# Low parts of weights by accumulating transfers onto ScalarE's negative, and a later place for a mean between two layers

## The chip, the cores and the metric

The kernel runs on one core of a Trainium2 chip. The metric is the device time of one execution in microseconds (us); the time of a kernel is the median of several executions.

## The reference

Two layers of an encoder, all in float32, with 512 tokens of width 1024 and 256 memory tokens:

```
for each layer:
  h   = rms_norm(x, g_pre)
  z   = h @ w_in                     # 1024 -> 5632: q, k, v of branches A and B, q of M, gates
  A   = neighborhood_attention(q, k, v, rpb)      # 6 heads, learned position bias rpb
  B   = dilated_attention(q, k, v)                # 3 groups of 2 heads, ALiBi distances
  M   = memory_attention(q, rms_norm(mem, mem_g), w_kv)
  y   = sigmoid-gated sum of A @ w_bra, B @ w_brb, M @ w_brm
  x   = x + rms_norm(y @ w_out, g_post)
  h   = rms_norm(x, g_pref)
  u   = gelu-gated MLP of h (w_up, a convolution of width 3 over positions, w_down)
  x   = x + rms_norm(u, g_postf)
```

rms_norm divides by the root of the mean of the squares over the 1024 channels.

## The kernel before

All activations are held transposed: channels on the 128 partitions, tokens along the free axis, in two halves of 256 tokens. A float32 product is made of three TensorE matmuls (`mm3`) in the type float32r: every operand is split into a high part (`hi`, the value rounded by ScalarE's copy) and a low part (`lo` = value - `hi`), and the product is hi x hi + hi x lo + lo x hi.

`weights` loads one block of a weight (1024 x 128, 512 KB) from DRAM on SyncE's queue into one of three buffers `wraw`. For blocks that are prepared ahead it then splits it in two chunks of 128 x 512 into tiles called `m`: ScalarE copies (`m<-wraw`, CAST) and an engine given by the argument `eng` subtracts (`m<-wraw,m`, L225 for GpSimd, L114 for VectorE: most of ScalarE's and VectorE's instructions have line 114, that of a wrapper that counts). In the names of the order lists below, m_71 and m_73 are the two high chunks of a block, m_72 and m_74 its low chunks.

GpSimd makes the low parts of three sets of blocks. In layer 0's first group, six blocks of w_in (`FIRST` = 0, 3, 4, 7, 6, 1), it makes the fourth and the sixth. Between the layers it makes those of the memory weights 2 and 3 (string `KVE`), and of the blocks 0, 1, 3 and 5 of layer 1's first group (string `GEN`; `G` is GpSimd, `V` VectorE); the first two of that group (`NG`) are prepared by the job `kv_ahead`, the others later.

TensorE's order is written out as the program is built: `Woven` keeps a clock that is an estimate in us, each matmul adds its cost, and jobs (generators) yield the time after which they want to go on; TensorE's instructions are chained in the order in which they are made. The other engines get their own instructions in an order that a scheduler chooses, each queue in order, with semaphores between them. GpSimd's queue holds its arithmetic and also the issue of its DMAs (a software queue): a DMA behind an instruction that waits is not issued before it.

The position bias of branch A is loaded by `a_bias` (L593 to L600), once for each head: a DMA of 128 KB on GpSimd's queue (`y<-in_rpb_dram`, L596), then three subtractions from a mask on GpSimd (`y<-mask,y`, L599). The load is held behind the last low part of a weight that GpSimd has made:

```
behind(nc.gpsimd.dma_start(out=raw, in_=rpb[l, h]).ins, last_lo.get(G))
```

`last_lo` is set in `split`, by the engine that subtracts. Its buffer is one of eight `y` tiles, which VectorE uses for the residual's product and for squares.

At the end of layer 0 (`end_job`, `raw_end_job`) the result of each half is normalised and added to the residual: transposes bring the statistics (`pt<-ident,st`), VectorE makes `y<-y,pt` and `x<-x,y` for eight channel blocks, ScalarE the squares of the new `x` (`sq<-x`), VectorE sums them (`acc<-acc,sq`), and TensorE takes their mean over channels by a matmul with a constant (`pt<-mean,acc`). For the second half, layer 1's first group of products goes on meanwhile with values that are not yet normalised (`ka`), and the mean's matmul stands among those products, where the job's `yield 3.5` puts it.

Of the kernel before, what the change touches and what calls it, by code (L numbers as in the profile page):

```python
# [9 lines left out]
AF = mybir.ActivationFunctionType  # L10
ALU = mybir.AluOpType
# [9 lines left out]
KD = D_MODEL // 128  # L21
# [6 lines left out]
FIRST = (0, 3, 4, 7, 6, 1)  # L28
# [6 lines left out]

LAT_QK, LAT_SM, LAT_T, LAT_V, LAT_T2 = 1.0, 4.5, 1.5, 2.0, 0.6
STEP_A, STEP_B, STEP_M = 9.0, 9.0, 5.5
SQG, LOG, GEN, KVE = {0: (), 1: ()}, {0: (), 1: ()}, 'GGVGVG', 'VVGG'
SD1 = 4.0
MARGIN = 0.3  # L40
SB = True
# [1 line left out]
KVD, GWD, NG, LAT1 = 7.3, 1.0, 2, 12.0  # L43
# [76 lines left out]
def tile_hybrid_encoder(ctx, tc, xT, memT, memg, vecs, rpb, w_in, w_kv, w_bra, w_brb, w_brm,  # L120
                        w_out, w_up, w_down, c_ident, c_mask, c_tab0, c_tab1, out):
    nc = tc.nc
# [13 lines left out]
    uid, last_copy, last_act, crit, last_lo = [0], [None], [None], [None], {}  # L136
    wv = Woven(tc)

    def nm(s):
        uid[0] += 1  # L140
        return f"{s}_{uid[0]}"


    def big(dt=F32R, shape=(128, 512)):
        return mp.tile(list(shape), dt, tag="m", name=nm("m"))
# [4 lines left out]
    def ktile(dt=F32R, shape=(128, 512)):  # L150
        return tp.tile(list(shape), dt, tag="ka", name=nm("ka"), bufs=12)
# [22 lines left out]
    def f32(ap):  # L174
        return ap.bitcast(F32)

    G = nc.gpsimd
    ACT, V = Counted(nc.scalar, wv, 0.1, 0.8e-3), Counted(nc.vector, wv, 0.065, 1.05e-3)

    DUP, MDUP = G, G  # L180
    MSQ = G

    def ready(least):
# [5 lines left out]
    def xh(k, half):  # L189
        return xs[:, half.start // 256, k, :]  # L190
# [27 lines left out]
    def behind(ins, other):  # L218

        if other is not None and ins is not other:  # L220
            tc.add_manual_dep(ins, other.name, ORDER, reason="issue order")

    def split(src, hi, lo, eng=None):
        last_copy[0] = ACT.copy(hi, src).ins
        last_lo[eng or V] = (eng or V).tensor_sub(lo, src, f32(hi)).ins  # L225

    def weights(src, K, C, slot=None, eng=None, after=None):

        raw = wp.tile([128, K, C], F32, tag="wraw", name=nm("wraw"))
        nc.sync.dma_start(out=raw, in_=src)  # L230
        if slot is None:
            hi = wp.tile([128, K, C], F32R, tag="whi", name=nm("whi"), bufs=2)
            lo = wp.tile([128, K, C], F32R, tag="wlo", name=nm("wlo"), bufs=2)
            split(raw, hi, lo, eng)
            behind(last_copy[0], after)
            return [(hi[:, k, :], lo[:, k, :]) for k in range(K)]
        n = 512 // C
        w = []
        for k in range(0, K, n):
            c = min(n, K - k)  # L240
            hi, lo = slot(F32R, (128, c, C)), slot(F32R, (128, c, C))
            split(raw[:, k:k + c, :], hi, lo, eng)
            w += [(hi[:, i, :], lo[:, i, :]) for i in range(c)]
        return w

# [68 lines left out]
    def sumsq_add(acc, src, first, slot=None, eng=None):  # L314
        if first:
            ACT.activation(acc, src, AF.Square)
        else:
            n = acc.shape[-1]
            sq = slot((128, 256)) if slot else small("sq2", 4) if n == 256 else small("sq", 1, (128, 512))
            ACT.activation(sq, src, AF.Square)  # L320
            (eng or V).tensor_add(acc, acc, sq)
# [4 lines left out]
    def rstd_job(accs, n, box):  # L326

        nb = n // 128
        bank = tbank((128, n + nb))
        pr, pt = bank[:, 0:n], bank[:, n:n + nb]  # L330
        for i, a in enumerate(accs):
            for b in range(nb):
                mm(pt[:, b:b + 1], a[:, 128 * b:128 * b + 128], mean, i == 0 and b == 0,
                   i == len(accs) - 1 and b == nb - 1, 0.11)
        rs = smalls(nb)
        crit[0] = ACT.activation(rs, pt, AF.Sqrt, bias=eps, scale=1.0).ins
        V.reciprocal(rs, rs)
        yield 0.8
        for b in range(nb):
            one = rs[:, b:b + 1]  # L340
            spread = bass.AP(one.tensor, one.offset, [list(one.ap[0]), [0, 128]])
            wv.pe(nc.tensor.transpose(pr[:, 128 * b:128 * b + 128], spread, ident), 0.11)
        box.append(pr)

    def normed(src, g, rs, hi, lo, eng=None):
        h32 = small("h32", 3)
        V.scalar_tensor_tensor(out=h32, in0=src, scalar=g, in1=rs, op0=ALU.mult, op1=ALU.mult)
        split(h32, hi, lo, eng)

    def raw_split(l, goff, k, src, hi, lo):  # L350

        g = vec[:, l, goff + k:goff + k + 1]
        ACT.activation(hi, src, AF.Copy, scale=g)
        V.scalar_tensor_tensor(out=lo, in0=src, scalar=g, in1=f32(hi), op0=ALU.mult, op1=ALU.subtract)

    def rtile():
        return tp.tile([128, 512], F32, tag="R", name=nm("R"), bufs=1)
# [60 lines left out]
    def raw_end_job(l, goff, og, acc, acc2, nxt, lat):  # L418


        half, box = HALVES[1], []
        hs, raw, R = nxt
        yield lat
        raw.extend((t[:, 0, :], t[:, 1, :]) for t in [ktile(F32R, (128, 2, 256)) for _ in range(KD)])
        yield from rstd_job([acc[:, half]], 256, box)
        for k in range(KD):
            V.tensor_mul(og[k][:, half], og[k][:, half], box[0])
            V.tensor_add(xh(k, half), xh(k, half), og[k][:, half])
            raw_split(l + 1, V_PRE, k, xh(k, half), *raw[k])
            if k == 0:  # L430
                yield 0.6
            wv.give(f"raw{k}")
            yield 1.05
        for k in range(KD):
            sumsq_add(acc2[:, half], xh(k, half), k == 0)
        yield 3.5
        box = []
        yield from rstd_job([acc2[:, half]], 256, box)
        ACT.copy(R[:, half], box[0])
        wv.give("R")  # L440
        for k in range(KD):
            normed(xh(k, half), vec[:, l + 1, V_PRE + k:V_PRE + k + 1], box[0], hs[k][0][:, half], hs[k][1][:, half])
        crit[0] = last_copy[0]
        yield 1.2
        wv.give(f"h{l + 1}.{V_PRE}.1")

    def h_tiles():
        return [(htile(), htile()) for _ in range(KD)]


    def mem_norm_job(l, hm, slot):
# [6 lines left out]
        for k in range(KD):  # L458
            sumsq_add(acc, raws[k], k == 0, None, MSQ if l else V)
        yield 14.0  # L460
# [34 lines left out]
    def group_weights(srcs, engs):  # L495
        return [weights(s, KD, 128, big, e) for s, e in zip(srcs, engs)]
# [19 lines left out]
    def proj(l, m, hs, after=None):  # L516
        w = weights(w_in[l, m], KD, 128, after=after)
        ps = mmbank()
        linear(ps, w, hs)
        return ps  # L520
# [366 lines left out]
    gw = group_weights([w_in[0, m] for m in FIRST[:2]], (V, V))  # L887
# [4 lines left out]
    with tc.issue_after(last_copy[0]):  # L892
        sqs = first_squares(HALVES[1])
    wv.spawn(pre_norm_job(0, V_PRE, sqs, hs, 1), SD1)
    gw += group_weights([w_in[0, m] for m in FIRST[2:]], (V, G, V, G))
    for t, c in ((mask, c_mask), (tab0, c_tab0), (tab1, c_tab1)):
        nc.sync.dma_start(out=t, in_=c)
    hm = []
# [3 lines left out]
    for l in range(depth):  # L902
# [41 lines left out]
        for m in range(KD):  # L944
# [3 lines left out]
            hi, lo = big(), big()  # L948
# [4 lines left out]
        hs, R, gw = h_tiles(), rtile(), []  # L953
# [44 lines left out]
        if l == depth - 1:  # L998
            sublayer_end(l, V_POSTF, w_of, fs, 2, None)
            while wv.jobs:  # L1000
                wv._step()
        else:
            hm, km, vm = [], [], []
            wv.spawn(mem_norm_job(l + 1, hm, htile), 20.0)
            pre, R, raw, box = [], rtile(), [], []

            def then(a, i, l=l, box=box):
                box.extend(h_tiles())
                return pre_norm_job(l + 1, V_PRE, a, box, i)

            gw = []

            def kv_ahead(l=l, pre=pre, gw=gw):
                pre.append(weights(w_kv[l + 1, 0], KD, 128, htile))
                yield KVD
                for i in (1, 2, 3):
                    yield 0.9
                    pre.append(weights(w_kv[l + 1, i], KD, 128, big, G if KVE[i] == 'G' else V))
                wv.give(f"kv{l + 1}")
                for m in range(NG):  # L1020
                    yield GWD
                    gw.extend(group_weights([w_in[l + 1, FIRST[m]]], [G if GEN[m] == 'G' else V]))
                wv.give(f"gw{l + 1}")

            sublayer_end(l, V_POSTF, w_of, fs, 1, [then, (box, raw, R)], (1.4, LAT1), lambda: wv.spawn(kv_ahead()))
            wv.need(f"kv{l + 1}")
            mem_kv(l + 1, hm, km, vm, pre)
            wv.need(f"gw{l + 1}")
            gw += group_weights([w_in[l + 1, m] for m in FIRST[NG:]], [G if e == 'G' else V for e in GEN[NG:]])
            wv.need(f"h{l + 1}.{V_PRE}.0")  # L1030
            hs = box

# [92 lines left out]
```

## Time and profile before

| what | value |
|---|---|
| median of 3 runs | 1551.14 us (1551.08 to 1551.52) |
| the profiled execution | 1551.73 us, its span 1550.0 us |
| mean granted TensorE clock in it | 0.995 |
| GpSimd's instructions and busy time | 217, 149.7 us |
| subtractions of weights on GpSimd near the start | 4, from 24.12 to 31.81 us |
| subtractions of weights on GpSimd between the layers | 8 from 768.30 to 780.85 us, 4 from 795.61 to 803.88 us |
| a bias load, from issue to landing | 2.3 least, 2.9 median, 7.0 most |

In the timeline rows of the profile the columns are the start in us, the length in us, the engine, the line, the operation with its tiles (written out<-in), the shape and how many instructions the row holds, and in brackets the idle time ahead of it with what ended it. PE is TensorE, DVE is VectorE, ACT is ScalarE, POOL is GpSimd and SP is SyncE. PEclk is the clock granted to TensorE, 1.00 being full speed.

### The profile page before, as it was taken

The page shows a single profiled execution, that of the slowest core. Times are in us where ns is not written, and L with a number is a line of the kernel's source. Part 1 is how long each engine was busy: PE and PEld are TensorE (multiplying, and loading weights), DVE is VectorE, ACT ScalarE, POOL GpSimd, SP SyncE. Part 2 cuts the span into 40 slices and gives each one's busy share as a digit, 9 for nine tenths or more (in the row PEclk, how much of TensorE's full clock was granted, in tenths as well). Part 3 has the DMA queues.
Part 4 walks back from the last instruction along what each step waited for, and adds up shares of the span by engine and source line. Part 5 has one row for each costly group of instructions (what it writes and reads, how often), then busy time and mean ns, then how long its engine had stood idle before and what let it go on. Part 6 is the DMA issues. An engine that isn't in the chain of part 4 may idle for free.

```text
span 1550.0 us, 20648 instructions
## 1 busy us (share of the span) xinstructions
PE 1522.5 (98%) x7970; PEld 1300.1 (84%) x7970; DVE 951.6 (61%) x1684; ACT 712.7 (46%) x1266; POOL 149.7 (10%) x217
## 2 busy tenths in 40 slices
PE   8999999999999999999989999999999999999997
PEld 7988888888988888888888888888889888888887
DVE  6685676335777777742497756753456977776233
ACT  5565554336544444532355555532354544444231
POOL 3340000110000000000154300002100000000000
PEclk9999999999999999999999999999999999999999
DMA  7221213235113322333431221132350233323331
GB/s 246 89 88 64 62 57 107 84 95 165 53 59 100 100 96 95 118 90 101 129 102 59 78 66 58 61 104 88 102 177 15 82 96 99 101 99 89 99 105 63
DMA packets 45810, 144.91 MB, mean 93 GB/s; under 512 B 5376, under 2 KB 9600, under 8 KB 45712
## 3 DMA queue, kind: packets, MB, share of 16 engines
q1 hardware_dynamic: 43776, 139.85, 28.5%
q10 hardware_dynamic: 1296, 2.10, 0.4%
q0 software_dynamic: 640, 1.64, 0.3%
q8 instruction: 62, 1.02, 0.3%
q14 instruction: 36, 0.29, 0.1%
HBM read 141.48 MB, written 2.10 MB: 93 GB/s over the span
## 4 chain that ended last, share of the span: by engine, by line
PE 91%; DVE 6%; ACT 2%; issue 1%; DMA 0%; SPq 0%; ACTq 0%; DVEq 0%
PE mm L247 80%; PE s L247 4%; PE o L247 3%; PE pt L258 2%; DVE m L114 1%; DVE y L114 1%; PE pt L247 1%; DVE ka L114 1%; DVE x L114 1%; ACT y L114 1%; DVE st L114 0%; DVE acc L114 0%; DMA x<-in_xT_dram 0%; DVE wlo L114 0%; ACT whi L114 0%
## 5 line engine op out<-in xcount | busy, mean ns | idle before, releaser
L247 PE MATMUL mm<-h,whi 128*128 128x512 f32 x2496 | 776.5, 392 | 0.0
L247 PEld LDWEIGHTS mm<-h,whi 128*128 128x128 f32 x2496 | 462.0, 188 | 91.3
L247 PE MATMUL mm<-h,wlo 128*128 128x512 f32 x1248 | 486.9, 390 | 0.0
L114 DVE TENSOR_TENSOR wlo<-wraw,whi 128x1024 fp32r<-128x1024 f32 (+1 forms) x213 | 259.2, 1217 | 284.7 <-ACT whi L114 282.3
L114 ACT CAST whi<-wraw 128x1024 fp32r<-128x1024 f32 (+1 forms) x213 | 221.4, 1040 | 307.8 <-PE mm L247 293.4
L247 PEld LDWEIGHTS mm<-h,wlo 128*128 128x128 f32 x1248 | 234.5, 188 | 49.6
L247 PE MATMUL mm<-m,whi 128*128 128x512 f32 (+1 forms) x800 | 215.1, 356 | 1.0 <-DVE m L114 0.8
L247 PEld LDWEIGHTS mm<-m,whi 128*128 128x128 f32 x800 | 141.8, 189 | 22.8 <-PE mm L247 1.3
L247 PE MATMUL mm<-m,wlo 128*128 128x512 f32 (+1 forms) x400 | 142.1, 355 | 0.0
L114 DVE SCALAR_TENSOR_TENSOR y<-y,vec,y 128x511 f32<-128x511 f32 x176 | 130.5, 748 | 3.5 <-ACT y L114 0.9
L114 DVE TENSOR_TENSOR y<-mm,R 128x512 f32<-128x512 f32 x82 | 56.4, 688 | 68.5 <-PE mm L247 68.5
L247 PEld LDWEIGHTS mm<-m,wlo 128*128 128x128 f32 x400 | 75.5, 189 | 10.9
L802 POOL TENSOR_TENSOR m<-m,y 128x512 f32<-128x512 f32 x28 | 36.1, 1289 | 399.4 <-DVE y L114 399.4
L114 ACT ACTIVATE y<-y,vec 128x512 f32<-128x512 f32 x88 | 71.1, 815 | 2.3 <-DVE y L114 1.9
L247 PE MATMUL mm<-m,m 128*128 128x512 f32 x240 | 63.5, 394 | 0.0
L114 ACT ACTIVATE y<-y 128x512 f32<-128x512 f32 x44 | 27.9, 633 | 71.7 <-DVE y L114 71.3
L114 ACT CAST m<-pt 128x512 fp32r<-128x512 f32 (+1 forms) x72 | 38.6, 541 | 46.8 <-PE pt L258 38.5
L114 ACT ACTIVATE y<-y,st 128x256 f32<-128x256 f32 (+1 forms) x80 | 43.8, 549 | 30.4 <-DVE st L114 28.9
L114 DVE TENSOR_TENSOR acc<-acc,sq 128x256 f32<-128x256 f32 (+1 forms) x80 | 41.1, 514 | 26.6 <-ACT sq L114 24.7
L114 DVE TENSOR_TENSOR m<-pt,m 128x512 fp32r<-128x512 f32 (+1 forms) x72 | 45.1, 630 | 19.9 <-ACT m L114 18.6
L114 ACT CAST m<-y 128x512 fp32r<-128x512 f32 x32 | 19.9, 622 | 72.5 <-DVE y L114 72.5
L247 PE MATMUL mm<-h,m 128*128 128x256 f32 x312 | 49.1, 301 | 2.0 <-ACT h L114 1.0
(154 smaller groups left out, 1789.9 us busy)
## 6 DMA issues: line engine op xcount, KB each, us to landing
wraw<-in_w_in_dram SPq DMA_DIRECT2D x88, 512.0 KB, 3.7
wraw<-in_w_up_dram SPq DMA_DIRECT2D x88, 512.0 KB, 3.6
wraw<-in_w_down_dram SPq DMA_DIRECT2D x32, 512.0 KB, 3.5
wraw<-in_w_out_dram SPq DMA_DIRECT2D x16, 512.0 KB, 3.9
wraw<-in_w_down_dram SPq DMA_DIRECT2D x16, 384.0 KB, 3.1
wraw<-in_w_kv_dram SPq DMA_DIRECT2D x8, 512.0 KB, 4.0
wraw<-in_w_bra_dram SPq DMA_DIRECT2D x16, 192.0 KB, 2.3
x<-in_xT_dram SPq DMA_DIRECT2D x8, 256.0 KB, 7.3
```

What stands on the lines that cost most here:

```text
L114: return op(*args, **kw)
L247: wv.pe(nc.tensor.matmul(ps, a, b, start=first, stop=last), cost)
L258: wv.pe(nc.tensor.transpose(ps[:, 128 * i:128 * i + 128], s, ident), 0.11)
L802: (V if br == 2 and m >= 6 else G).tensor_add(acc[m], acc[m], gs)
```

## The change

A third way to make a low part, `'D'`: ScalarE writes the negative of the high part into the low tile (it rounds in the same way), and a DMA of GpSimd's software queue adds the weight to it, read a second time from DRAM (`accum_op=ALU.add`, 256 KB, two for each block). It is used for the blocks that GpSimd subtracted, with small exchanges: in layer 0's first group the last two blocks (6 and 1) are made so and block 7 goes to VectorE; between the layers it is memory weights 2 and 3 and the blocks 0, 1, 4 and 5 of the group, and blocks 2 and 3 are VectorE's. The second edit is `yield 5.0` for `yield 3.5` in `raw_end_job`. Since `split` is not called with GpSimd any more, `last_lo` has no entry for it at the places of the change.

```diff
-SQG, LOG, GEN, KVE = {0: (), 1: ()}, {0: (), 1: ()}, 'GGVGVG', 'VVGG'
+SQG, LOG, GEN, KVE = {0: (), 1: ()}, {0: (), 1: ()}, 'DDVVDD', 'VVDD'
...
+    ENG = {'G': G, 'V': V, 'D': 'D'}
...
             hi, lo = slot(F32R, (128, c, C)), slot(F32R, (128, c, C))
-            split(raw[:, k:k + c, :], hi, lo, eng)
+            if eng == "D":
+                last_copy[0] = ACT.copy(hi, raw[:, k:k + c, :]).ins
+                ACT.activation(lo, raw[:, k:k + c, :], AF.Copy, scale=-1.0)
+                nc.gpsimd.dma_start(out=lo, in_=src[:, k:k + c, :], accum_op=ALU.add)
+            else:
+                split(raw[:, k:k + c, :], hi, lo, eng)
...
         for k in range(KD):
             sumsq_add(acc2[:, half], xh(k, half), k == 0)
-        yield 3.5
+        yield 5.0
...
-    gw += group_weights([w_in[0, m] for m in FIRST[2:]], (V, G, V, G))
+    gw += group_weights([w_in[0, m] for m in FIRST[2:]], (V, V, 'D', 'D'))
...
-                    pre.append(weights(w_kv[l + 1, i], KD, 128, big, G if KVE[i] == 'G' else V))
+                    pre.append(weights(w_kv[l + 1, i], KD, 128, big, ENG[KVE[i]]))
...
-                    gw.extend(group_weights([w_in[l + 1, FIRST[m]]], [G if GEN[m] == 'G' else V]))
+                    gw.extend(group_weights([w_in[l + 1, FIRST[m]]], [ENG[GEN[m]]]))
...
-            gw += group_weights([w_in[l + 1, m] for m in FIRST[NG:]], [G if e == 'G' else V for e in GEN[NG:]])
+            gw += group_weights([w_in[l + 1, m] for m in FIRST[NG:]], [ENG[e] for e in GEN[NG:]])
```

GpSimd's queue near the start, before (m_62 to m_64 are the low chunks of block 7, m_72 and m_74 those of block 1; y_164 and y_180 receive the bias of heads 0 and 1):

```order
L225 TENSOR_TENSOR m_62_255<-wraw_60_252,m_61_254 128x512
L225 TENSOR_TENSOR m_64_259<-wraw_60_252,m_63_258 128x512
L225 TENSOR_TENSOR m_72_275<-wraw_70_272,m_71_274 128x512
L225 TENSOR_TENSOR m_74_279<-wraw_70_272,m_73_278 128x512
L596 DMA y_164_925<-in_rpb_dram 128x256
L599 TENSOR_TENSOR y_163_924<-mask_106,y_164_925 128x256 x2
L599 TENSOR_TENSOR y_164_925<-mask_106,y_164_925 128x256
L596 DMA y_180_1008<-in_rpb_dram 128x256
L599 TENSOR_TENSOR y_179_1007<-mask_106,y_180_1008 128x256 x2
L599 TENSOR_TENSOR y_180_1008<-mask_106,y_180_1008 128x256
```

And after (lines are 6 higher; m_67 and m_69 are the low chunks of block 6, L246 is the accumulating DMA):

```order
L602 DMA y_164_929<-in_rpb_dram 128x256
L605 TENSOR_TENSOR y_163_928<-mask_106,y_164_929 128x256 x2
L605 TENSOR_TENSOR y_164_929<-mask_106,y_164_929 128x256
L602 DMA y_180_1012<-in_rpb_dram 128x256
L246 DMA m_67_265<-in_w_in_dram 128x512
L246 DMA m_69_270<-in_w_in_dram 128x512
L605 TENSOR_TENSOR y_179_1011<-mask_106,y_180_1012 128x256 x2
L605 TENSOR_TENSOR y_180_1012<-mask_106,y_180_1012 128x256
L246 DMA m_72_277<-in_w_in_dram 128x512
L246 DMA m_74_282<-in_w_in_dram 128x512
```

The bias of two heads, loads and subtractions, stood behind the weights' low parts and now stands ahead of those of block 1; the two DMAs of block 6 stand behind the second load and ahead of its subtractions.

TensorE's order at the place where these tiles are read, after (it is that of before, with other numbers; the first of these rows is the first `s<-h,m` matmul of the first group):

```order
L253 MATMUL s_79_293<-h_3_112,m_66_264 128x256
L253 MATMUL s_79_293<-h_4_113,m_66_264 128x256
L253 MATMUL s_79_293<-h_3_112,m_67_265 128x256
L253 MATMUL s_80_294<-h_3_112,m_71_276 128x256
L253 MATMUL s_80_294<-h_4_113,m_71_276 128x256
L253 MATMUL s_80_294<-h_3_112,m_72_277 128x256
```

Block 6's first low chunk is read by the third of these matmuls and block 1's by the sixth; the second chunks are read four channel blocks later.

GpSimd's queue between the layers, for the last blocks of layer 1's first group, before (m_1405 and m_1407 are block 3's low chunks of the group, m_1415 and m_1417 block 5's):

```order
L225 TENSOR_TENSOR m_1405_7245<-wraw_1403_7242,m_1404_7244 128x512
L225 TENSOR_TENSOR m_1407_7249<-wraw_1403_7242,m_1406_7248 128x512
L225 TENSOR_TENSOR m_1415_7265<-wraw_1413_7262,m_1414_7264 128x512
L225 TENSOR_TENSOR m_1417_7269<-wraw_1413_7262,m_1416_7268 128x512
L596 DMA y_1472_7760<-in_rpb_dram 128x256
L599 TENSOR_TENSOR y_1471_7759<-mask_106,y_1472_7760 128x256 x2
L599 TENSOR_TENSOR y_1472_7760<-mask_106,y_1472_7760 128x256
L596 DMA y_1486_7843<-in_rpb_dram 128x256
```

And after (m_1410 and m_1412 are block 4's low chunks):

```order
L602 DMA y_1472_7776<-in_rpb_dram 128x256
L246 DMA m_1410_7267<-in_w_in_dram 128x512
L246 DMA m_1412_7272<-in_w_in_dram 128x512
L605 TENSOR_TENSOR y_1471_7775<-mask_106,y_1472_7776 128x256 x2
L246 DMA m_1415_7279<-in_w_in_dram 128x512
L605 TENSOR_TENSOR y_1472_7776<-mask_106,y_1472_7776 128x256
L246 DMA m_1417_7284<-in_w_in_dram 128x512
L602 DMA y_1486_7859<-in_rpb_dram 128x256
```

Here too the bias load of a head comes first now, and two of its subtractions stand ahead of block 5's first DMA.

TensorE's order around the second half's mean, before:

```order
L247 MATMUL mm_1418_7272<-ka_1426_7298,m_1350_7003 128x256 x2
L247 MATMUL mm_1418_7272<-ka_1426_7298,m_1351_7004 128x256
L247 MATMUL mm_1419_7273<-ka_1426_7298,m_1355_7025 128x256 x2
L247 MATMUL mm_1419_7273<-ka_1426_7298,m_1356_7026 128x256
L247 MATMUL pt_1443_7516<-mean_96,acc_1202_6081 128x1 x2
L247 MATMUL mm_1418_7272<-ka_1427_7299,m_1350_7003 128x256 x2
```

And after:

```order
L253 MATMUL mm_1418_7288<-ka_1428_7316,m_1352_7016 128x256 x2
L253 MATMUL mm_1418_7288<-ka_1428_7316,m_1353_7017 128x256
L253 MATMUL mm_1419_7289<-ka_1428_7316,m_1357_7040 128x256 x2
L253 MATMUL mm_1419_7289<-ka_1428_7316,m_1358_7041 128x256
L253 MATMUL pt_1443_7544<-mean_96,acc_1202_6085 128x1 x2
L253 MATMUL mm_1418_7288<-ka_1429_7317,m_1352_7016 128x256 x2
```

The mean's matmuls stand behind the products of the fifth channel block (`ka_1428`) instead of the third (`ka_1426`), twelve matmuls later.

## The prediction

> **What bounds the kernel now.** I read the page first for the span, the busy shares and the chain of waits, then TensorE's waits, then the timelines of the two places that the change touches. On the page, section 1 and the chain's shares by engine:
>
> ```profile
> span 1550.0 us, 20648 instructions
> PE 1522.5 (98%) x7970; PEld 1300.1 (84%) x7970; DVE 951.6 (61%) x1684; ACT 712.7 (46%) x1266; POOL 149.7 (10%) x217
> PE 91%; DVE 6%; ACT 2%; issue 1%; DMA 0%; SPq 0%; ACTq 0%; DVEq 0%
> ```
>
> TensorE is busy for 1522.5 of 1550.0 us, and the chain runs through it for 91%. Neither its work nor that of any long stretch is touched by the change, so only TensorE's idle time can move: 27.5 us in all, plus time at a lower clock. The profiled execution took 1551.73 us, 0.6 above the median of 1551.14; I make differences in it and set them on the median. The largest of TensorE's waits, and its timeline, PEclk beside it in windows of 4 us (columns: window, length, busy and count of PE, PEld, DVE, ACT, POOL, granted clock, DMA share, GB/s):
>
> ```profile
> PE pt L247 <- DVE acc L114: 4.6, 2, 3.5
> ...
> 777.09 3.04 PE L247 MATMUL mm<-h,m 128*128 128x256 f32 x24
> 783.59 0.58 PE L247 MATMUL pt<-mean,acc 128*128 128x1 f32 x4 [3.46 <-DVE acc L114]
> ...
> 813.64 0.58 PE L247 MATMUL pt<-mean,acc 128*128 128x1 f32 x4 [1.16 <-DVE acc L114]
> ...
> 873.12 0.55 PE L258 MATMUL pt<-ident,y 128*128 128x128 f32 x3 [2.09 <-DVE y L114]
> ...
> 784.00:788.00 4.00, 3.90 (x22) 3.61 (x22) 3.14 (x9) 2.06 (x6) 3.07 (x8) 0.60 0.02 4
> 812.00:816.00 4.00, 2.84 (x25) 2.67 (x24) 1.44 (x4) 0.26 (x1) 3.41 (x8) 1.00 0.10 30
> 874.00:878.00 4.00, 4.00 (x17) 3.28 (x16) 2.20 (x3) 2.42 (x4) 1.30 (x3) 0.63 0.03 3
> ```
>
> Between the layers TensorE waits twice for VectorE's sums of squares, 3.46 and 1.16 us. After the first the clock falls to 0.60 for a window, which costs 0.40 x 4.00 = 1.6 us. After an idle of 2.09 us it falls too (0.63), after 1.16 it does not (1.00). The wait of 2.09 lies in code that the change leaves in order, and stays.
>
> **What the change takes away between the layers.** Sixteen subtractions leave GpSimd; eight run just where VectorE sums the first half's squares:
>
> ```profile
> 768.30 6.93 POOL L225 TENSOR_TENSOR m<-wraw,m 128x512 fp32r<-128x512 f32 x5 [105.56 <-ACT m L114]
> 776.61 4.24 POOL L225 TENSOR_TENSOR m<-wraw,m 128x512 fp32r<-128x512 f32 x3 [1.39 <-ACT m L114]
> ...
> 770.41 2.22 DVE L114 TENSOR_TENSOR x<-x,y 128x256 f32<-128x256 f32 x2
> 773.22 0.85 DVE L114 TENSOR_TENSOR acc<-acc,sq 128x256 f32<-128x256 f32 x1
> 774.00 1.85 DVE L114 TENSOR_TENSOR x<-x,y 128x256 f32<-128x256 f32 x2
> 776.88 1.40 DVE L114 TENSOR_TENSOR acc<-acc,sq 128x256 f32<-128x256 f32 x1
> 778.87 0.86 DVE L114 TENSOR_TENSOR acc<-acc,sq 128x256 f32<-128x256 f32 x1
> 779.65 1.83 DVE L114 TENSOR_TENSOR x<-x,y 128x256 f32<-128x256 f32 x2
> 782.40 0.41 DVE L114 TENSOR_TENSOR acc<-acc,sq 128x256 f32<-128x256 f32 x1
> 783.02 0.76 DVE L114 TENSOR_TENSOR acc<-acc,sq 128x256 f32<-128x256 f32 x2 [0.21 <-ACT sq L114]
> ...
> 806.21 0.75 DVE L114 TENSOR_TENSOR x<-x,y 128x256 f32<-128x256 f32 x2
> ```
>
> Beside GpSimd's subtractions a pair of `x<-x,y` takes 2.22, 1.85 and 1.83 us, and alone 0.75; an `acc<-acc,sq` takes 0.85, 1.40 and 0.86, and alone 0.41. The excess is 1.47 + 1.10 + 1.08 + 0.44 + 0.99 + 0.45 = 5.5 us. The last sum ends at 783.02 + 0.76 = 783.8, so without it at 778.3. TensorE comes at 777.09 + 3.04 = 780.1. ScalarE's eight added negatives stand between the squares, and about 1.8 us of delay fits under that; each is priced by ScalarE's copy of the same tile (0.55 us, row below), 4.4 us in all, of which ScalarE's gaps while it waits for VectorE hide most. So the 3.46 us and the half clock behind it go. Swapping two of VectorE's subtractions at the start costs nothing (two gained, two lost). For the second mean, the matmuls move two steps of six matmuls later, 12 x 0.12 = 1.4 us (48 matmuls take 5.92 us in the row at 31.23 below), against a wait of 1.16, which goes. Gain: 3.46 + 1.6 + 1.16 = 6.2 us.
>
> **What it adds: the software queue stands in line.** GpSimd's bias loads were held behind its last subtraction of a weight. That holder is gone, so the loads and the bias subtractions, which wait for them, now stand ahead of or among the accumulating transfers on GpSimd's queue. At the start the order after is: bias load, three subtractions, bias load, two transfers (w_in block 6), three subtractions, two transfers (block 1). Rows for it:
>
> ```profile
> 16.80 0.42 SPq L897 DMA_DIRECT2D mask<-in_c_mask_dram  x1
> mask<-in_c_mask_dram SPq DMA_DIRECT2D x1, 384.0 KB, 6.1
> ...
> 21.28 2.54 DVE L114 TENSOR_TENSOR y<-y,y 128x256 f32<-128x256 f32 x6
> 24.79 1.65 ACT L114 CAST m<-wraw 128x512 fp32r<-128x512 f32 x3
> 28.90 2.91 POOL L225 TENSOR_TENSOR m<-wraw,m 128x512 fp32r<-128x512 f32 x2 [2.08 <-ACT m L114]
> 31.23 5.92 PE L247 MATMUL s<-h,m 128*128 128x256 f32 x48
> 44.14 2.12 POOL L599 TENSOR_TENSOR y<-mask,y 128x256 f32<-128x256 f32 x3 [2.46 <-DMA y<-in_rpb_dram]
> ...
> DMA to landing us min/median/max: 2.3/2.9/7.0
> m<-in_memT_dram ACTq DMA_DIRECT2D x4, 256.0 KB, 5.8
> y<-in_rpb_dram POOLq DMA_DIRECT2D x2, 128.0 KB, 4.9
> 22.00:26.00 4.00, 3.14 (x27) 2.94 (x26) 2.52 (x7) 3.40 (x10) 1.88 (x2) 1.00 0.23 74
> 26.00:30.00 4.00, 4.00 (x36) 4.00 (x35) 3.61 (x9) 2.75 (x7) 1.92 (x2) 1.00 0.75 241
> ```
>
> The row of landings is that of the bias loads (128 KB, software queue). No accumulating transfer is in the trace of before. A price for its 256 KB: at least a bias load's median, 2.9 us, at most the 5.8 us that 256 KB of memory tokens took in this loaded stretch; I take the middle, 4.35, because the DMA engines are 0.75 busy here. A bias load in quiet traffic I take at 2.9 (0.23 busy at 22 to 26), in loaded traffic at 3.6, halfway from 2.9 to 4.35; bounds 2.3 and 7.0. Three bias subtractions take about 2.1 to 2.3 us (2.12).
>
> Start, step by step. The first load waits for the first of the six `y<-y,y` at 21.28 (its buffer): 21.7. Landing 21.7 + 2.9 = 24.6; the mask is there at 16.80 + 6.1 = 22.9. Three subtractions to 26.9. Second load, in loaded traffic, 30.5. Three subtractions to 32.8. Only then is the transfer for block 1 issued: 32.8 + 4.35 = 37.15. The negatives are not late: ScalarE ends the copies behind them about where GpSimd's subtractions began before (28.90). Before, those subtractions ended at 31.81 and TensorE did not wait. It wants this tile at its sixth matmul of the run at 31.23, that is 31.23 + 5 x 0.12 = 31.8. Wait: 37.15 - 31.8 = 5.3 us, and, since an idle of 2.09 us lowered the clock, 1.6 more: +6.9. All of it lies on TensorE's path, since the waits left after it are for engines that stall with it. Bounds: with 2.9 for every transfer, 21.7 + 2.9 + 2.1 + 2.9 + 2.1 + 2.9 = 34.6, a wait of 2.8; with 7.0 for the second load and 5.8 for the transfer, and the first at 4.9 like the two bias loads between 14 and 50, 21.7 + 4.9 + 2.3 + 7.0 + 2.3 + 5.8 = 44.0, a wait of 12.2. The two issues of block 6's transfers (0.56 each by the bias load's row at 810.73 below) go out while the second load is under way and cost nothing. The four negatives here, 2.2 us, fill ScalarE's 0.60 and 1.25 us of idle time in the two windows; the 0.35 left over is covered by TensorE's wait, and would show without it. SP's queue keeps its order; a raw buffer is given back after ScalarE's second read instead of after a subtraction, no later than before.
>
> Between the layers, for the last weight of layer 1's first group:
>
> ```profile
> 795.53 0.43 PE L342 MATMUL pt<-ident,st 128*128 128x128 f32 x2
> 796.00 0.75 DVE L114 TENSOR_TENSOR y<-y,pt 128x256 f32<-128x256 f32 x2 [0.52 <-PE pt L342]
> 796.66 0.79 DVE L114 TENSOR_TENSOR m<-wraw,m 128x512 fp32r<-128x512 f32 x1
> ...
> 804.44 5.92 PE L247 MATMUL s<-h,m 128*128 128x256 f32 x48
> 810.73 0.56 POOL L596 DMA_DIRECT2D y<-in_rpb_dram  x1
> 813.20 2.27 POOL L599 TENSOR_TENSOR y<-mask,y 128x256 f32<-128x256 f32 x3
> ```
>
> The bias load now comes first and waits for the second half's first `x<-x,y`, which frees its buffer: 796.00 + 0.4 for the product, 0.6 for a weight's subtraction (0.79 beside GpSimd's), 0.4, so 797.4 on before's clock. Landing at 3.6: 801.0; two bias subtractions, 1.75: 802.75; the accumulating transfer 4.35: 807.1. TensorE wants that tile at 804.44 + 5 x 0.12 = 805.0. Wait 2.1, with 1.6 for the clock: +3.7. Bounds: 797.4 + 2.9 + 1.4 + 2.9 = 804.6, no wait; with 7.0 and 5.8, 811.9, a wait of 6.9. The other accumulating transfers are ahead of their readers by more than this. The memory they read again adds 16 x 256 KB = 4 MB to 145; nothing there is short of bandwidth outside the start.
>
> The Trainium skill, "TensorE: Matmul & The Clock Gate", Part 1, has the clock fall only after an idle window of about 3.4 us; by it a wait of 2.1 us would cost no clock, and the sum would be 1.6 less. The trace fell after 2.09 (0.63 in the row above), and I go by that.
>
> **The sum.** +6.9 + 3.7 - 6.2 = +4.4: 1551.14 + 4.4 = 1555.5 us. Changes under 0.2% (3.1 us) a measurement here can hardly tell from none, so slower begins at 1554.2 and faster at 1548.0.
>
> **Rivals.**
> A, faster: software-queue transfers land as quickly as the bias load issued at 810.73, whose readers ran at 813.20 without waiting, 2.5 us at most, the accumulating ones too. Start: 21.7 + 2.5 + 2.1 + 2.5 + 2.1 + 2.5 = 33.4, a wait of 1.6, too short to lower the clock; between the layers none. Net 1.6 - 6.2 = -4.6: 1546.5. It is decided by the landing: at about 2.9 each the start passes 2.09 and the clock falls. For it speaks that row, against it the 0.75 load and the maximum of 7.0. The Trainium skill, "DMA: Bandwidth & Descriptors", Anatomy of one DMA — SWDGE (gpsimd) path, fits 2.0 us + bytes / 436e3, an estimate of 2.3 us for 128 KB and 2.6 for 256; with it the start's wait is 1.3 and the time 1546.2. The trace's 2.3 minimum agrees, its median of 2.9 and its 7.0 don't.
> B, within 0.2%: every landing at 2.9: 2.8 + 1.6 + 0 - 6.2 = -1.8: 1549.3. A start wait up to 5 us with no boundary wait belongs here.
> C, clearly slower: the transfers queue behind the weight loads as the slowest bias load did (7.0): 12.2 + 1.6 + 6.9 + 1.6 - 6.2 = +16.1: 1567.
> D, the gain fails: ScalarE's negatives delay the squares by more than 1.8 us, so that about 2 us of the wait stays with its clock loss, 3.6 less gain: 1559.1. Against it: VectorE, not ScalarE, is late there in the rows above.
>
> **How the numbers follow.** My sum and its neighbours (4.4 plus or minus 2) 0.34, D 0.08, C 0.12, B 0.26, A 0.20. Slower: 0.34 + 0.08 + 0.12 = 0.54, less 0.02 for the lower edge, 0.52; same 0.26 + 0.02 = 0.28; faster 0.20. The range leaves out A's lower tail and the far half of C: 1546.3 to 1563.0; the slower cases alone would span 1554.2 to 1563.0.
>
> **What would show it.** Right: a TensorE wait of about 5 us for a DMA (`m` from w_in) near 31.8, clock below 1 behind it; GpSimd's transfers standing behind bias subtractions; no wait at `pt<-mean,acc`; pairs of `x<-x,y` at 0.75 near 770; a short wait in the run of `s<-h,m` between the layers. Wrong: landings near 2.5 us, or `pt<-mean,acc` still waiting for VectorE.

## The result and the profile after

The changed kernel takes 1564.68 us (median of 4 runs, 1563.1 to 1564.94) against 1551.33 us for the kernel before on the same chip. The ratio is 1.008, 95% interval 1.0063 to 1.0098: slower by 10 to 15 us, where 1555.5 was forecast and 1563.0 was the end of the range.

The page of the kernel after, its span, DMA queues (packets, MB, share of the time of 16 engines) and the chain's shares:

```profile
span 1563.2 us, 20680 instructions
q1 hardware_dynamic: 43776, 139.85, 28.2%
q0 software_dynamic: 2944, 5.84, 1.9%
...
PE 90%; DVE 4%; DMA 2%; issue 2%; ACT 1%; POOL 1%; SPq 0%; POOLq 0%; ACTq 0%
```

DMA has come onto the chain, with 2%. TensorE's waits (in total, how many, the longest), with the landings of GpSimd's transfers into `m` (the accumulating ones):

```profile
PE s L253 <- DMA m<-in_w_in_dram: 13.1, 4, 5.2
PE mm L253 <- DMA m<-in_w_in_dram: 1.0, 1, 1.0
...
DMA to landing us min/median/max: 4.2/8.7/10.8
```

The waits for `pt<-mean,acc` are gone from the list and 14.1 us of waits for transfers stand in it. Their places, in TensorE's timeline with GpSimd's queue, and windows of the start:

```profile
31.14 0.40 PE L253 MATMUL s<-h,m 128*128 128x256 f32 x2
35.02 1.01 PE L253 MATMUL s<-h,m 128*128 128x256 f32 x3 [3.48 <-DMA m<-in_w_in_dram]
41.24 6.80 PE L253 MATMUL s<-h,m 128*128 128x256 f32 x43 [5.21 <-DMA m<-in_w_in_dram]
...
24.81 2.58 POOL L605 TENSOR_TENSOR y<-mask,y 128x256 f32<-128x256 f32 x3 [2.29 <-DMA y<-in_rpb_dram]
27.34 0.56 POOL L602 DMA_DIRECT2D y<-in_rpb_dram  x1
27.90 1.85 POOL L246 DMA_DIRECT2D m<-in_w_in_dram  x2
33.05 2.26 POOL L605 TENSOR_TENSOR y<-mask,y 128x256 f32<-128x256 f32 x3 [3.29 <-DMA y<-in_rpb_dram]
35.25 1.76 POOL L246 DMA_DIRECT2D m<-in_w_in_dram  x2
...
32.00:36.00 4.00, 0.98 (x3) 0.72 (x3) 1.97 (x4) 0.80 (x2) 2.96 (x5) 0.77 1.02 261
36.00:40.00 4.00, 0.03 (x1) 0.00 (x0) 0.83 (x2) 1.69 (x6) 1.01 (x2) 0.50 1.08 346
40.00:44.00 4.00, 2.76 (x13) 2.76 (x14) 3.48 (x8) 2.86 (x5) 0.00 (x0) 0.50 0.46 83
```

The queue stands as forecast: bias, subtractions, bias, block 6, subtractions, block 1. But block 6's first transfer, issued at 27.90, is there only at 35.02 (7.1 us), and block 1's, issued at 35.25, at 41.24 (6.0). The DMA engines are full meanwhile (1.02 and 1.08). Between the layers:

```profile
791.08 0.50 PE L253 MATMUL pt<-mean,acc 128*128 128x1 f32 x4
...
799.67 1.82 PE L253 MATMUL mm<-h,m 128*128 128x256 f32 x13 [0.96 <-DMA m<-in_w_in_dram]
812.57 0.63 PE L253 MATMUL s<-h,m 128*128 128x256 f32 x3 [0.67 <-DMA m<-in_w_in_dram]
816.97 7.90 PE L253 MATMUL s<-h,m 128*128 128x256 f32 x43 [3.77 <-DMA m<-in_w_in_dram]
824.71 3.71 PE L253 MATMUL mm<-ka,m 128*128 128x256 f32 x30
828.26 0.50 PE L253 MATMUL pt<-mean,acc 128*128 128x1 f32 x4
...
781.52 0.75 DVE L114 TENSOR_TENSOR x<-x,y 128x256 f32<-128x256 f32 x2
...
804.94 0.57 POOL L602 DMA_DIRECT2D y<-in_rpb_dram  x1 [9.42 <-DVE x L114]
810.13 2.68 POOL L605 TENSOR_TENSOR y<-mask,y 128x256 f32<-128x256 f32 x2 [2.83 <-DMA y<-in_rpb_dram]
812.75 0.87 POOL L246 DMA_DIRECT2D m<-in_w_in_dram  x1
```

The two means at 791.08 and 828.26 (before at 783.59 and 813.64) don't wait any more, and `x<-x,y` is back at 0.75 a pair. Against the timeline before, the same instructions start later by: 10.9 us after the start's products (`mm<-h,m` at 47.88, before 36.99), 11.1 at 788.20, 5.9 at 796.65 (`s<-ident,m`, before 790.72; the first wait and its low clock gone, gain 5.2), 7.1 at 802.66, and 14.5 at 824.71 (before 810.20). The span ends 13.2 later: the second mean has given 1.3 back. So +10.9 - 5.2 + 1.2 + 7.4 - 1.3 = +13.0 of 13.2; the 0.2 left came between 47.88 and 788.20.

### The profile page after: what moved, and what is told of

Read it like the earlier page. It is cut to its first block, busy times and chain, and to the rows that moved or that the text cites. A ratio compares the mean times of both kernels' runs of the same rounds, so it can differ in the third digit from the quotient of the medians.

```text
span 1563.2 us, 20680 instructions
## 1 busy us (share of the span) xinstructions
PE 1526.2 (98%) x7970; PEld 1303.5 (83%) x7970; DVE 942.7 (60%) x1684; ACT 717.5 (46%) x1282; POOL 143.4 (9%) x217
## 3 DMA queue, kind: packets, MB, share of 16 engines
q1 hardware_dynamic: 43776, 139.85, 28.2%
q8 instruction: 62, 1.02, 0.3%
## 4 chain that ended last, share of the span: by engine, by line
PE 90%; DVE 4%; DMA 2%; issue 2%; ACT 1%; POOL 1%; SPq 0%; POOLq 0%; ACTq 0%
PE mm L253 79%; PE s L253 5%; PE o L253 3%; PE pt L264 2%; DVE m L114 1%; DVE y L114 1%; DMA y<-in_rpb_dram 1%; PE pt L253 1%; DMA m<-in_w_in_dram 1%; DVE ka L114 0%; DMA wraw<-in_w_in_dram 0%; DMA x<-in_xT_dram 0%; ACT y L114 0%; DVE wlo L114 0%; DVE st L114 0%
## 5 line engine op out<-in xcount | busy, mean ns | idle before, releaser
L253 PEld LDWEIGHTS mm<-m,wlo 128*128 128x128 f32 x400 | 75.5, 189 | 10.9
L253 PE MATMUL s<-h,m 128*128 128x256 f32 x336 | 52.0, 303 | 13.1 <-DMA m<-in_w_in_dram 13.1
L253 PEld LDWEIGHTS s<-h,m 128*128 128x128 f32 x336 | 47.2, 209 | 14.0 <-DMA m<-in_w_in_dram 14.0
```

The costliest lines, as they stand in the source:

```text
L253: wv.pe(nc.tensor.matmul(ps, a, b, start=first, stop=last), cost)
```

## The experiments

The changes of each are against the kernel named; ratios are to the kernel before, on the same chip.

**The parts alone.** First the later mean in the kernel before.

```diff
-        yield 3.5
+        yield 5.0
```

> The kernel before with the later place of the second half's mean alone. Theory: the 1.16 us wait at that mean goes, the place itself costs nothing: 1.0 to 1.3 us faster, 1550.1. Rival: the mean of the squares leads to the normalised second half, which then comes later by 1.4 us and is waited for: no gain, 1551.3 or up to 0.3 above.

Measured: 1548.51 us, ratio 0.9985 (0.9977 to 0.9994): faster by 1 to 3.6 us. In its trace the wait of 3.5 at the first mean is left and the second has none. The theory's 1.0 to 1.3 lies in the interval; the place costs nothing.

Then the changed kernel with the other parts taken back, once all but the start, once the start:

```diff
-SQG, LOG, GEN, KVE = {0: (), 1: ()}, {0: (), 1: ()}, 'DDVVDD', 'VVDD'
+SQG, LOG, GEN, KVE = {0: (), 1: ()}, {0: (), 1: ()}, 'GGVGVG', 'VVGG'
-        yield 5.0
+        yield 3.5
```

> Only layer 0's first group is made by accumulating transfers (four of them); between the layers all is as before. Theory: the whole loss of the start, two waits of 3.5 and 5.2 us and the low clock behind them, is caused there and is carried to the end: +10.9, 1562.2. Rival: half of it is given back by later waits that the delay covers: 1557.

```diff
-    gw += group_weights([w_in[0, m] for m in FIRST[2:]], (V, V, 'D', 'D'))
+    gw += group_weights([w_in[0, m] for m in FIRST[2:]], (V, G, V, G))
```

> The start as before; between the layers everything as in the changed kernel, the later mean included. Theory: the gain at the two means (5.2 and 1.3 us) is lost again to the waits for the group's last low parts (1.2 and 7.4 us): +2.1 to +2.5, 1553.7. Rival: those waits came only because the start had shifted the traffic: 1546 or less.

Measured: start alone 1564.75, ratio 1.0088 (1.0074 to 1.0101); between the layers alone 1553.13, ratio 1.0012 (1.0003 to 1.0021). The start alone lost 11 to 16 us, somewhat more than the 10.9 expected; in its trace TensorE is 11.9 us late at 48.86 and 12.9 at the end. So the loss is carried to the end in full and given back nowhere. The stretch between the layers, gain and loss together, is about level (+1.9), and its waits come without the start's as well. The two parts add up to 15.5 us against 12.4 for the whole change, which the intervals allow. TensorE's waits in the second:

```profile
789.20 1.81 PE L253 MATMUL mm<-h,m 128*128 128x256 f32 x13 [1.59 <-DMA m<-in_w_in_dram]
802.28 0.62 PE L253 MATMUL s<-h,m 128*128 128x256 f32 x3 [0.87 <-DMA m<-in_w_in_dram]
806.40 8.00 PE L253 MATMUL s<-h,m 128*128 128x256 f32 x43 [3.49 <-DMA m<-in_w_in_dram]
```

**The place in the queue, and the price of a transfer.** Two suspected causes, each taken away alone, then both. The place: `last_lo` is set by the transfers, so the bias loads are held behind them.

```diff
-                nc.gpsimd.dma_start(out=lo, in_=src[:, k:k + c, :], accum_op=ALU.add)
+                last_lo[G] = nc.gpsimd.dma_start(out=lo, in_=src[:, k:k + c, :], accum_op=ALU.add).ins
```

> The changed kernel with each bias load held behind the last accumulating transfer, so that GpSimd's queue has the order weights, then bias, as before the change. If the place in the queue is what costs: start 27 us issue instead of 28 for block 6 and 29.5 instead of 35.2 for block 1, the second wait is gone at the start (+4 to +6 instead of +10.9) and the last transfers between the layers are issued at 804 to 808 instead of 805 to 815, wait 0 to 2 instead of 4.4: 1552 to 1556. If the transfers' own landing (6 to 7 us in full traffic) is what costs, the four at the start, now issued close together, share the queue and end as late: 1560 to 1565.

The price: the same transfers without the addition.

```diff
-                nc.gpsimd.dma_start(out=lo, in_=src[:, k:k + c, :], accum_op=ALU.add)
+                nc.gpsimd.dma_start(out=lo, in_=src[:, k:k + c, :])
```

> The changed kernel with plain transfers in place of the accumulating ones: the low tile receives the weight itself, so the subtraction is left out; same queue, bytes, issues and waits. Theory (an accumulating packet holds a DMA engine about twice as long as a plain one): packets of the software queue shorter by 40 to 50%, landing 3 to 4.5 us instead of 6 to 7, start +6 to +7, 1555 to 1557. Rival (it is the software queue and the second read, not the accumulation): landing and time as in the changed kernel, 1563 to 1565.

Both edits:

> The changed kernel with plain transfers (the subtraction left out) and the bias loads held behind them: both suspected costs taken away together. If price and place in the queue are two causes that add up, block 1's transfer is issued at 29 and lands near 34, a wait of about 2 at the start (with the clock +3.5), the last ones between the layers land in time or 1 us late, and the gain at the means (6.5) shows: 1548 to 1551. If there is a third cost (the four extra reads of ScalarE, the second reading of the memory), it stays at 1553 or above.

| transfers | bias ahead | bias behind |
|---|---|---|
| accumulating | 1.0080 (1.0063 to 1.0098) | 1.0070 (1.0056 to 1.0084) |
| plain | 1.0035 (1.0021 to 1.0049) | 1.0004 (0.9994 to 1.0014) |

Without the addition 7 us of the 12.4 go (0.0045 x 1551), without the bias ahead 1.6, which the intervals can't tell from nothing, and without both 11.8. The price is the larger cause. Medians: 1561.82 with the bias behind (at the upper end of what the second theory gave), 1555.47 plain, 1552.20 with both, which is 1 us above what two causes alone were to give. The 6.5 us gained at the means are in all four, so some 7 us of loss are left even with both edits: TensorE still waits 0.42 and 2.39 us at the start and 3.09 between the layers (shown below), with a low clock behind, since plain transfers too land in 5.8 us there and not in 4.7. The expectation had the last ones in time or 1 us late. A third cost is not needed for this, and not excluded. The place is worth 4.8 us once the transfers are plain (1.0035 to 1.0004), and hardly counts while they are dear: with the bias behind, block 1's first transfer is issued at 29.02 instead of 35.25, but TensorE gets it only 2.3 us earlier (38.90 instead of 41.24), and waits 2.04 and 4.18 instead of 3.48 and 5.21. Of the kernel with the bias behind, then of the plain one, then of the one with both: TensorE's waits at the start (of the last also the one between the layers), and GpSimd's landings. The rows of the plain kernel are of an execution of 1560.46 us, 5.0 above its median, so they show less of the gain than the ratio does.

```profile
33.71 1.01 PE L253 MATMUL s<-h,m 128*128 128x256 f32 x3 [2.04 <-DMA m<-in_w_in_dram]
38.90 7.62 PE L253 MATMUL s<-h,m 128*128 128x256 f32 x43 [4.18 <-DMA m<-in_w_in_dram]
DMA to landing us min/median/max: 7.3/9.7/10.8
```

```profile
q0 software_dynamic: 2944, 5.84, 1.3%
33.09 1.01 PE L253 MATMUL s<-h,m 128*128 128x256 f32 x3 [2.26 <-DMA m<-in_w_in_dram]
38.88 7.23 PE L253 MATMUL s<-h,m 128*128 128x256 f32 x43 [4.79 <-DMA m<-in_w_in_dram]
DMA to landing us min/median/max: 3.9/4.7/5.8
```

```profile
30.70 0.62 PE L253 MATMUL s<-h,m 128*128 128x256 f32 x3 [0.42 <-DMA m<-in_w_in_dram]
33.70 6.91 PE L253 MATMUL s<-h,m 128*128 128x256 f32 x43 [2.39 <-DMA m<-in_w_in_dram]
806.62 6.84 PE L253 MATMUL s<-h,m 128*128 128x256 f32 x43 [3.09 <-DMA m<-in_w_in_dram]
DMA to landing us min/median/max: 4.6/5.8/8.6
```

In like orders the addition takes the landing from a median of 4.7 to 8.7 us, and from 5.8 to 9.7. The queue's packets show a part of the reason: with the same number and bytes, the software queue holds 16 engines for 1.9% of the span when it adds and for 1.3% when it doesn't, against 0.3% before:

```profile
q0 software_dynamic: 640, 1.64, 0.3%
```

For the 4.2 MB of the change that is 25 us against 16; the 139.85 MB of the weight loads take 28.2%, 441 us. So 6.0 us for each MB with the addition, 3.7 without, 3.2 for a plain weight load (shares are given to 0.1%, so plus or minus 0.4 in the first two). The records of the packets in the traces of these two, the changed kernel and the plain one, are finer: a packet of 2,048 bytes took 178 ns in the median with the addition and 99 ns without, all of them together 23.8 and 13.8 us of 16 engines. For one transfer that is 1.5 against 0.9 us, a difference of 0.6; the landings differ by 4. How the rest comes about among the other loads is not shown.

**Fewer transfers, and transfers in another stage.** The kernel before with block 1 of the first group alone made so (the other three of the four V, G, V), bias loads behind:

```diff
-    gw += group_weights([w_in[0, m] for m in FIRST[2:]], (V, G, V, G))
+    gw += group_weights([w_in[0, m] for m in FIRST[2:]], (V, G, V, 'D'))
```

> The kernel before with only block 1 of layer 0's first group made by accumulating transfers (two instead of four), the bias loads behind them, block 7 on GpSimd as before. If the landing grows with the accumulating bytes that share the DMA engines, it is 5 to 6 us from an issue at 29: wait 2.5 to 3.5, 1555 to 1557. If an accumulating transfer takes its 7 to 10 us in any case, wait 5 or more: 1558 to 1561. If only the crowd of four made it long: 1552 or less.

Measured: 1559.41, ratio 1.0046 (1.0031 to 1.0061). Two transfers instead of four and nothing ahead of them, and yet they land after 8.6 to 9.4 us:

```profile
28.88 1.92 POOL L246 DMA_DIRECT2D m<-in_w_in_dram  x2 [2.84 <-ACT m L114]
37.51 6.70 PE L253 MATMUL s<-h,m 128*128 128x256 f32 x43 [6.30 <-DMA m<-in_w_in_dram]
DMA to landing us min/median/max: 8.6/9.0/9.4
32.00:36.00 4.00, 0.00 (x0) 0.00 (x0) 1.22 (x4) 0.66 (x2) 0.00 (x0) 0.70 0.95 262
```

So it is not the crowd of the four that makes them long; two beside the loads of the memory and its weights, with the engines at 0.95, are enough. Then eight transfers of 256 KB in another stage of the kernel before, `w_brm`'s low parts:

```diff
-                wb = weights(w_brm[l, m // 2], 2, 256, big)
+                wb = weights(w_brm[l, m // 2], 2, 256, big, 'D')
```

> The price by itself: the kernel before with the low parts of the third branch's weights (w_brm, four blocks in each layer, 256 KB each) by one accumulating transfer each, in a stage where the DMA engines are mostly idle. If the long landings come from full DMA engines: 3.5 to 5 us here, and 16 engines' share per transfer still 1.5 us. If an accumulating transfer is slow in itself: 6 us or more. The time: hidden by the blocks' lead, 1551, or up to 4 us more where a block is read at once.

Measured: 1590.3 us, ratio 1.0248 (1.023 to 1.0266). The expected lead was not there: six of the eight were waited for, 24.6 us in all, and the mean granted clock fell from 0.995 to 0.983, which is where the rest of the 38 us is likely to lie (it was not followed row by row). The landings, the window of the first from its issue at 289.00, and what they cost TensorE:

```profile
DMA to landing us min/median/max: 4.9/5.2/5.9
289.00:294.00 5.00, 5.00 (x24) 4.14 (x23) 1.82 (x2) 1.35 (x2) 2.20 (x2) 1.00 0.89 211
PE mm L253 <- DMA m<-in_w_brm_dram: 24.6, 6, 4.3
```

The stage was not quiet where it mattered: weight loads of SyncE's queue run beside each of the eight, and in the 5.2 us from their issues the engines are 0.73 to 0.89 busy, the transfers' own packets included. So an accumulating transfer of 256 KB takes 4.9 to 5.9 us in this traffic, and up to 10.8 in that of the changed kernel. The 5.2 lies between the two outcomes that were expected and decides for neither; why it is 9 at the start with the engines at 0.95 is not shown. What such a transfer takes alone was not measured, and only this size was tried.

**Does the gain between the layers need the transfers?** The start as before in all of these, the mean late; against the changed kernel. The last four blocks of the group V, G, V, G, or all on VectorE, the early ones by transfer:

```diff
-SQG, LOG, GEN, KVE = {0: (), 1: ()}, {0: (), 1: ()}, 'DDVVDD', 'VVDD'
+SQG, LOG, GEN, KVE = {0: (), 1: ()}, {0: (), 1: ()}, 'DDVGVG', 'VVDD'   # the first
+SQG, LOG, GEN, KVE = {0: (), 1: ()}, {0: (), 1: ()}, 'DDVVVV', 'VVDD'   # the second
```

> The start as before, and between the layers accumulating transfers only for memory weights 2 and 3 and the group's first two blocks; the other four go V, G, V, G as before, the mean stays late. Theory: keeps the gain at the two means (5.2 and 1.3) and has only the wait of about 1 us for the group's first blocks: 1546. Rival: GpSimd's four subtractions stretch VectorE's sums of the second half again, and the eight transfers in a row land no earlier: 1549 to 1551.

> As the one before, with the group's last four blocks all on VectorE, so GpSimd makes no low part between the layers. Theory: VectorE's operations there get shorter by what GpSimd no longer disturbs, which pays for four more subtractions of 0.6 us: 1545 to 1547. Rival: VectorE, busy all of 796 to 812, comes late with the second half's sums or with block 5: 1548 to 1552.

Measured: 1543.96, ratio 0.9957 (0.9944 to 0.9969), and 1544.84, ratio 0.9962 (0.9949 to 0.9974). Both faster, by 4 to 9 us, as the theory had it (the first 2 us more than it said). Then with no transfer at all, the early ones on VectorE too, and with GpSimd out of it altogether between the layers:

```diff
-SQG, LOG, GEN, KVE = {0: (), 1: ()}, {0: (), 1: ()}, 'DDVVDD', 'VVDD'
+SQG, LOG, GEN, KVE = {0: (), 1: ()}, {0: (), 1: ()}, 'VVVGVG', 'VVVV'   # the first
+SQG, LOG, GEN, KVE = {0: (), 1: ()}, {0: (), 1: ()}, 'VVVVVV', 'VVVV'   # the second
```

> As the version with V, G, V, G for the last four blocks, but the eight early low parts between the layers on VectorE too, so no accumulating transfer is left. If taking work off VectorE and GpSimd in 768 to 780 is what pays, eight subtractions of 0.6 us put VectorE's first sum back to 783 and the wait of 2 to 3.5 with its clock loss is there again: 1548 to 1550. If only GpSimd's disturbance of VectorE mattered: 1544 to 1546.

> The start as before, the mean late, and every low part between the layers on VectorE: neither GpSimd nor an accumulating transfer makes any. If what paid is that GpSimd no longer subtracts beside VectorE, VectorE's four more subtractions (2.6 us) are paid for by its undisturbed operations at 795 to 812 and the wait of 1.96 at the second half's mean falls to under 1: 1543.5 to 1546. If VectorE is now full there, that wait grows to 3 or more: 1547 to 1550.

Measured: 1545.81, ratio 0.9961 (0.9946 to 0.9976), and 1545.34, ratio 0.9960 (0.9947 to 0.9973). The four versions can't be told apart. The expectation that eight subtractions of 0.6 us would put VectorE's first sum back to 783 was wrong: its timeline in the first of these two (no transfer) shows why, with TensorE's means.

```profile
766.47 1.89 DVE L114 TENSOR_TENSOR m<-wraw,m 128x512 fp32r<-128x512 f32 x3 [0.45 <-ACT m L114]
769.68 0.76 DVE L114 TENSOR_TENSOR x<-x,y 128x256 f32<-128x256 f32 x2
776.02 0.70 DVE L114 TENSOR_TENSOR m<-wraw,m 128x512 fp32r<-128x512 f32 x1
778.54 0.42 DVE L114 TENSOR_TENSOR acc<-acc,sq 128x256 f32<-128x256 f32 x1
779.23 0.50 PE L253 MATMUL pt<-mean,acc 128*128 128x1 f32 x4
811.13 0.58 PE L253 MATMUL pt<-mean,acc 128*128 128x1 f32 x4 [1.96 <-DVE acc L114]
812.00:816.00 4.00, 4.00 (x23) 4.00 (x23) 0.95 (x3) 0.65 (x3) 0.00 (x0) 0.61 0.00 0
```

The first subtractions fit ahead of the residual's work and others between the sums; the last sum ends at 779.0 and the mean at 779.23 doesn't wait, with the pair of `x<-x,y` at 0.76. With GpSimd's early subtractions left and the same late mean (the first experiment) the ratio was 0.9985 (0.9977 to 0.9994), just above the intervals of all four versions here. So for the early blocks what paid is that GpSimd no longer subtracts beside VectorE, and not where the subtraction went. For the last four blocks it does matter: all by transfer gave 1.0012 (1.0003 to 1.0021). No version without GpSimd's early subtractions was run with the mean early.

## Why the prediction was wrong

The direction (given a chance of 0.52) and the mechanisms were right, the size was not: +4.4 forecast, +12 to +13 found. Of the 8.6 us between the sum and the trace's 13.0, 4.0 arose at the start (+10.9 for +6.9) and 4.9 between the layers (+8.6 for +3.7), and the gain was 0.3 larger. Point by point:

- **The gain.** 6.2 forecast (3.46 + 1.6 + 1.16); 5.2 + 1.3 = 6.5 in the trace. Right, with its reason: the pairs of `x<-x,y` at 0.75. ScalarE's negatives did not delay the sums (rival D is out).
- **The queue at the start.** First load forecast at 21.7, landed 24.6; it was 21.90 and 24.81. From there the steps part: the second load landed at 33.05 (forecast 30.5) and block 1's transfer at 41.24 (37.15).
- **The failed terms: the landings in loaded traffic, a bias load "in loaded traffic at 3.6" and an accumulating transfer at 4.35.** At the start the second bias load was issued 0.4 us later than forecast and took 5.6 us to land, 2.0 too long, and block 1's transfer took 6.0, 1.6 too long: together about 4 us, by which it came late (41.24 for 37.15). Of the transfer's price, "at least a bias load's median, 2.9 us, at most the 5.8 us that 256 KB of memory tokens took", even the upper bound was too low: first chunks took 6.0 and 7.1 at the start, and the median over the kernel was 8.7. In the plain kernel block 1's transfer took 4.4 (34.49 to 38.88), as forecast; so this term missed the addition. But the bias load took 5.3 there too, so that one missed the traffic. The trace of before had it: the load issued at 31.76, with the engines 0.75 to 0.88 busy, took 7.0, and the 4.9 in the prediction's rows is the median of this one and of one that took 2.9.

```profile
y<-in_rpb_dram POOLq DMA_DIRECT2D x1, 128.0 KB, 7.0
```

- **The range.** The prediction's own upper bounds held, 44.0 for block 1's transfer (found 41.24) and 811.9 between the layers (found 816.97 - 7.1 = 809.9); the range ended at 1563.0 and left most of that side out.
- **Block 6.** The sum had it in time (its transfers "cost nothing"); it was waited for 3.48 us. With a landing of 4.35 from 27.90 it would have come at 32.25, with a wait of 0.7: that too is the price. The wait lies inside block 1's delay, since TensorE would have stood until 41.24 for that one in any case.
- **The clock.** 1.6 for each stretch forecast. At the start 10.9 - 8.7 = 2.2; between the layers 7.4 - 4.4 = 3.0, where 43 matmuls took 7.90 us (48 took 5.92 before). It is not a fixed cost: behind waits of 3.1 to 3.8 us between the layers the same 43 matmuls took 6.8 to 8.0 us in this kernel, in the one with the new start left out, and in those with plain transfers or the bias behind.
- **Between the layers.** The first bias load was issued where it was forecast (804.94 - 7.1 = 797.8, forecast 797.4), was followed by its subtractions after 5.2 us instead of 3.6, and two of these took 2.68 instead of 1.75. Block 5's transfer then took 4.2 (812.75 to 816.97), as forecast, so here the price was not what failed. The wait was 4.4 instead of 2.1. An added wait of 0.96 at 799.67, for the group's first blocks, stood under "ahead of their readers by more than this": with eight accumulating transfers one behind the other it was not.
- **"Nothing there is short of bandwidth outside the start".** Not so: with the eight transfers the DMA engines were full between the layers from 784 to 796. The prediction counted 4 MB more of 145, by bytes; by the engines' time it is nearly twice that (6.0 against 3.2 us for each MB). A window of the changed kernel, then the one in the kernel before with the same place in the program:

```profile
788.00:792.00 4.00, 3.92 (x33) 3.84 (x33) 1.38 (x4) 3.83 (x10) 2.06 (x3) 1.00 1.09 293
```

```profile
776.00:780.00 4.00, 4.00 (x35) 3.92 (x33) 3.96 (x8) 2.19 (x6) 3.39 (x3) 1.00 0.37 119
```

- **The rivals.** A (landing as fast as the shortest bias load) needed 2.5 us for an accumulating transfer; the shortest landing in the changed kernel is 4.2. The Trainium skill, "DMA: Bandwidth & Descriptors", Anatomy of one DMA — SWDGE (gpsimd) path, gives by its fit an estimate of 2.6 us for 256 KB; the plain transfers' least here is 3.9 and their median 4.7, and the accumulating ones' 5.2 with the engines 0.73 to 0.89 busy. All of these share the engines with other loads, so for this kernel's traffic the measurements decide, and no run here shows the fit's own case. C had a part of the cause (transfers behind weight loads in full engines; the addition is the other) and its 1567 is nearer to the result than the sum.

On the clock the Trainium skill, "TensorE: Matmul & The Clock Gate", Part 1, has it fall after an idle window of about 3.4 us; here it fell after idles of 1.96 (the row at 811.13 above, 0.61 behind it) and 2.09, and not after 1.59 (1.00 behind it) and 1.16. So an idle well under that figure was enough in this kernel.

## What to carry to other kernels

A DMA that adds is not a plain DMA of the same bytes: price it from a run, by its landing in the traffic of its place and by the engines' time that it takes from the loads beside it. A transfer on a compute engine's queue is late by everything in front of it, but look for the price first: here the order cost 1.6 us (within the noise) with the dear transfers and 4.8 with plain ones, the price 7 to 10. A median of few landings can hide the one that counts: look for the load that ran in the same stretch. When a change pays by what it removes, try the removal with the plainest replacement; VectorE's own subtractions, with the later mean, gave the same 6 us as the early transfers between the layers, and needed no transfer.

## What the runs showed of the hardware

- An accumulating transfer of the software queue held the DMA engines about 1.7 times as long as the same transfer without the addition (23.8 to 13.8 us of 16 engines for 4.2 MB; 178 to 99 ns for a packet of 2,048 bytes), and landed in 4.9 to 5.9 us (256 KB) with the engines 0.73 to 0.89 busy, in up to 10.8 in the changed kernel's traffic (up to 1.09).
- GpSimd needed 0.86 to 0.89 us in the median to issue an accumulating transfer (changed kernel, bias behind, `w_brm`), against 0.53 to 0.55 us for the plain one of the same shape.
- VectorE's pair of `x<-x,y` took 1.83 to 2.22 us beside GpSimd's subtractions and 0.75 to 0.76 without them.
- In this kernel, where TensorE is busy for 98% of the span, a stall at the start was carried to the end undiminished over 1500 us (with the changed start alone +11.9 at 48.86 us and +12.9 at the end).
